# Memory norm on rows, four chunks of seven products in the first values unit, queries turned by DMA, two changes of order

## The chip, the cores and the metric

The kernel runs on one core of a Trainium2 chip. A core has a matrix engine (TensorE; in the profile PE, and PEld for its weight loads), a vector engine (VectorE, DVE), a scalar engine (ScalarE, ACT), a general engine (GpSimd, POOL) and a queue engine (SyncE, SP) that issues DMA transfers. The metric is the time of one execution on the device in microseconds (us), as a median of several runs.

## The reference

One decoder layer, batch 1, 256 tokens, width 2048, all in fp32:

```
h = x + 0.5 * SwiGLU_1(rmsnorm(x))                  # 2048 -> 5632 -> 2048
z = rmsnorm(h) @ w_in                               # columns u, v (1024 each), q (1024), k and v of the window (256)
h = h + concat(rmsnorm(gate(u, v)), rmsnorm(window_attention(q, k, v))) @ w_out
kv = rmsnorm(mem, g_mem) @ w_xkv                    # memory of 256 rows: keys 2048, values 2048
h = h + cross_attention(rmsnorm(h) @ w_xq, kv) @ w_xo
h = h + 0.5 * SwiGLU_2(rmsnorm(h))
out = rmsnorm(h)

rmsnorm(x, g) = x * rsqrt(mean(x*x, -1) + 1e-5) * g
```

The factor `rsqrt(mean(mem*mem)+eps)` is one number for each row of the memory. It can multiply the normalised memory before the product with `w_xkv`, or the rows of the product behind it.

## The kernel before, in words

**Products.** Each fp32 operand is split into a high part (fp32r) and the rest: ACT casts the high part, DVE subtracts it to get the low part (`split`, L146 to L148). A product of two such operands is three matmuls: high by high, low by high, high by low. In the names of the profile `wh` and `wl` are high and low parts of a weight, `th` and `tl` those of sums of weights, `fh` and `fl` those of a pair of the left operand.

**Units and chunks.** A projection of 256 tokens onto 1024 columns is a *unit*: 2 x 2 output blocks of 128 tokens by 512 columns, each a PSUM bank, over the 2048 rows of the weight. The weight comes in 8 *chunks* of 256 rows (1 MB, `load`, L347). A chunk is a product of 2 x 2 by 2 x 2 blocks and comes in kinds. `N` and `C` use eight block products (24 matmuls, L447); `S` uses Strassen's seven (21 matmuls) on sums of the blocks of both operands. The left operand's blocks and sums lie in a `Pair` (L190). The sums of the weight's blocks (`t`, L356 to L360) are made by DVE for each `S` chunk. Kind `D` is a pair with the sums of both `S` and `C`, so that one unit may use it as the one and another unit as the other; its extra forms are called `more`.

**Order on PE.** PE's order is the order of the program. `push` (L513) loads a chunk and hands its matmuls to `turn` (L505), which first issues the matmuls of the chunk before (`flush`), so that loading and splitting run one chunk ahead. `turn` then calls the functions in `later` whose count is 0, and counts the rest down. Functions in `side` (norms, transposes, attention) are generators that `side_step` continues between every six matmuls.

**Order on the other engines.** ACT, DVE, POOL and SP instructions are ordered by a planner that goes by the order of the program and by when it expects each operand. Every engine then runs its instructions in that order and waits at the head. Weights wait for one of three raw buffers and one of two `wh` and `wl` buffers; a DMA on SP's queue holds up those behind it while it waits for its source.

**Places that the change touches.**

- First layer, start: `first_pair` (L906) makes pairs of `n1` from raw rows of x transposed: ACT scales the rows (L936) and casts, DVE subtracts (L148). The pair's sums (`sums`, L924, `fill_sums`, L272) aren't wanted before the second unit; they are put off by `later`.
- Queries: `late_q` (L982) scales the rows of the query projection, `queries` (L990) turns them on PE with 16 transposes in the stage of the window's keys and values (`narrow_unit`, L551; 96 matmuls of 256 columns at L571) and copies four banks. `attend` (L1077) needs them after.
- Memory norm: `beside_queries` sums the squares of the memory's rows; `spread` (L1009) turns the factor of each row into a tile `by_token` that has it along the free dimension, by a product with a matrix of ones. `pair_normalized` (L306) multiplies the transposed memory by gain and `by_token` on DVE, for eight pairs `mT`.
- Memory values and keys: units `mv0`, `mv1` (L1255, L1259) and `mk0`, `mk1` (L1307). Their seven-product chunks are closed by `seven_early` and `seven_late` (L593, L601) on DVE, which write the rows.
- Output projection of the cross attention: `added_unit("xo", ...)` (L676), twice, with side work that turns the next norm's input through PSUM banks of the pool `tr`. Its seven-product chunks open the banks P1, Q5, Q6 and Q7 in the same pool.
- `turned_rows` (L150), used elsewhere already: ACT copies rows so that the two 16-bit halves of each word stand apart, a transposing DMA on SP's queue turns them, and ACT joins the halves afterwards.

## Time and profile before

| | |
|---|---|
| median of 3 runs | 2025.03 us (2024.72 to 2027.14) |
| profiled execution | 2024.46 us, its span 2022.8 us |
| PE busy | 2007.2 us, 9165 matmuls recorded |
| PEld, DVE, ACT busy | 82%, 92%, 65% of the span |
| granted clock of PE | 0.999 |
| mean DMA rate | 206 GB/s |

Starts of stages on PE, in us: first layer 6; query projection 694; keys and values 739; v 753; u 800; first values 853, second 906; keys 952 and 995; output of the mixer 1038; cross queries 1127; cross output 1228; second layer 1331 to 2014.

A row of time has start, duration, engine, line, operation, output and inputs, shapes, and in brackets how long the engine was idle before it and for what. A matmul's duration overlaps the next one's, so distances between starts tell the pace. A group row has count, total busy time and the mean of one in ns. A row of windows has, for each engine, busy time and number of instructions.

### The profile page before, as it was taken

What the parts mean: (1) busy time and instruction counts of PE and PEld (TensorE: products, weight loads), DVE (VectorE), ACT (ScalarE), POOL (GpSimd) and SP (SyncE); (2) the same over time, 40 slices, a digit from 0 to 9 for tenths busy, and PEclk for the clock granted to TensorE, in tenths of its full rate; (3) what the DMA queues carried; (4) which work ended last, traced back from release to release, by engine and by line L of the source; (5) the groups of instructions that cost most, each with busy time, mean ns of one, the idle gap of its engine ahead of it and who ended that gap; (6) DMA issues with size and microseconds to landing.
All of it is one profiled execution on the core that took longest, in us unless ns stands there. A gap on an engine that the chain in (4) does not pass through costs nothing.

```text
span 2022.8 us, 24182 instructions
## 1 busy us (share of the span) xinstructions
PE 2007.2 (99%) x9165; PEld 1665.3 (82%) x9165; DVE 1859.3 (92%) x1993; ACT 1305.5 (65%) x1442; POOL 34.0 (2%) x57
## 2 busy tenths in 40 slices
PE   9999999999999999999999999999999999999998
PEld 7888888888888888888888888888888888888886
DVE  7999999989999978988878977899999999999998
ACT  7656666667765766655556676675666665676664
POOL 0000000000000010100000000000000000000000
PEclk9999999999999999999999999999999999999999
DMA  8676657666555565545665544456576657565563
GB/s 313 202 242 208 222 207 234 214 218 219 191 205 208 189 227 198 185 159 187 210 217 185 203 150 151 177 188 235 194 236 221 224 196 242 203 219 203 189 227 125
DMA packets 115333, 415.83 MB, mean 206 GB/s; under 512 B 61824, under 2 KB 63888, under 8 KB 68112
## 3 DMA queue, kind: packets, MB, share of 16 engines
q1 hardware_dynamic: 112768, 407.14, 57.5%
q0 software_dynamic: 2016, 6.30, 1.0%
q8 instruction: 72, 1.18, 0.2%
q10 hardware_dynamic: 432, 0.84, 0.1%
q14 instruction: 45, 0.37, 0.1%
HBM read 398.52 MB, written 2.10 MB: 198 GB/s over the span
## 4 chain that ended last, share of the span: by engine, by line
PE 73%; DVE 3%; issue 1%; ACT 1%; POOL 0%; POOLq 0%; DVEq 0%
PE f2gQ L447 16%; PE f2dQ L447 6%; PE f1dQ L447 6%; PE f2gP L447 6%; PE xqQ L447 3%; PE f2dP L447 3%; PE f1dP L447 3%; PE woQ L447 2%; PE xoQ L447 2%; PE f2dR L447 2%; PE f1dR L447 2%; PE mv0Q L447 2%; PE vQ L447 2%; PE mv1Q L447 2%; PE mk1Q L447 2%; PE mk0Q L447 2%
## 5 line engine op out<-in xcount | busy, mean ns | idle before, releaser
L147 ACT CAST f2gwh<-f2gw 128x1536 fp32r<-128x1536 f32 (+1 forms) x88 | 150.6, 1712 | 76.0 <-PE f2gQ L447 58.8
L147 ACT CAST f1gwh<-f1gw 128x1536 fp32r<-128x1536 f32 (+2 forms) x94 | 152.1, 1622 | 67.4 <-PE f1gQ L447 51.9
L148 DVE TENSOR_TENSOR f1gwl<-f1gw,f1gwh 128x1536 fp32r<-128x1536 f32 (+2 forms) x94 | 181.4, 1931 | 14.3 <-ACT f1gwh L147 14.1
L148 DVE TENSOR_TENSOR f2gwl<-f2gw,f2gwh 128x1536 fp32r<-128x1536 f32 (+1 forms) x88 | 179.4, 2040 | 6.7 <-ACT f2gwh L147 6.6
L447 PE MATMUL f2gQ<-f2gwh,n4fh 128*128 128x512 f32 x317 | 123.6, 390 | 0.0
L447 PE MATMUL f2gQ<-f2gwh,n4fl 128*128 128x512 f32 x317 | 123.4, 389 | 0.0
L447 PE MATMUL f1gQ<-f1gwh,n1fl 128*128 128x512 f32 x315 | 122.7, 389 | 0.0
L447 PE MATMUL f1gQ<-f1gwh,n1fh 128*128 128x512 f32 x315 | 122.6, 389 | 0.0
L147 ACT CAST f2gth<-f2gt 128x1024 fp32r<-128x1024 f32 x82 | 85.1, 1049 | 57.8 <-DVE f2gt L356 29.4
L147 ACT CAST f1gth<-f1gt 128x1024 fp32r<-128x1024 f32 x78 | 81.1, 1049 | 60.5 <-DVE f1gt L356 30.7
L147 ACT CAST f2dwh<-f2dw 128x2048 fp32r<-128x2048 f32 (+1 forms) x44 | 77.4, 1758 | 48.0 <-PE f2dQ L447 43.2
L147 ACT CAST f1dwh<-f1dw 128x2048 fp32r<-128x2048 f32 (+1 forms) x44 | 77.4, 1758 | 41.0 <-PE f1dQ L447 37.3
L148 DVE TENSOR_TENSOR f1dwl<-f1dw,f1dwh 128x2048 fp32r<-128x2048 f32 (+1 forms) x44 | 92.3, 2098 | 11.4 <-ACT f1dwh L147 11.2
L148 DVE TENSOR_TENSOR f2dwl<-f2dw,f2dwh 128x2048 fp32r<-128x2048 f32 (+1 forms) x44 | 92.3, 2097 | 11.0 <-ACT f2dwh L147 10.7
L148 DVE TENSOR_TENSOR f2gtl<-f2gt,f2gth 128x1024 fp32r<-128x1024 f32 x82 | 99.8, 1221 | 1.3 <-ACT f2gth L147 0.3
L447 PE MATMUL f2gQ<-f2gwl,n4fh 128*128 128x512 f32 x317 | 96.7, 390 | 0.0
L447 PE MATMUL f1gQ<-f1gwl,n1fh 128*128 128x512 f32 x315 | 96.4, 390 | 0.0
L148 DVE TENSOR_TENSOR f1gtl<-f1gt,f1gth 128x1024 fp32r<-128x1024 f32 x78 | 95.2, 1221 | 1.1
L447 PE MATMUL f1gP<-f1gwh,n1fl 128*128 128x512 f32 x176 | 68.8, 391 | 2.2 <-DVE n1fl L148 2.1
L447 PEld LDWEIGHTS f2gQ<-f2gwh,n4fl 128*128 128x128 f32 x317 | 59.5, 188 | 12.3
L447 PEld LDWEIGHTS f2gQ<-f2gwh,n4fh 128*128 128x128 f32 x317 | 59.5, 188 | 12.3
L447 PEld LDWEIGHTS f2gQ<-f2gwl,n4fh 128*128 128x128 f32 x317 | 59.4, 188 | 12.3
(790 smaller groups left out, 6026.2 us busy)
## 6 DMA issues: line engine op xcount, KB each, us to landing
f2gw<-in_w_gu SPq DMA_DIRECT2D x88, 1024.0 KB, 4.9
f1gw<-in_w_gu SPq DMA_DIRECT2D x86, 1024.0 KB, 5.1
f1dw<-in_w_down SPq DMA_DIRECT2D x44, 1024.0 KB, 4.8
f2dw<-in_w_down SPq DMA_DIRECT2D x44, 1024.0 KB, 4.8
wow<-in_w_out SPq DMA_DIRECT2D x16, 1024.0 KB, 4.9
xqw<-in_w_xq SPq DMA_DIRECT2D x16, 1024.0 KB, 4.8
xow<-in_w_xo SPq DMA_DIRECT2D x16, 1024.0 KB, 4.8
qw<-in_w_in SPq DMA_DIRECT2D x8, 1024.0 KB, 4.7
```

The source lines that it names most:

```text
L147: nc.scalar.copy(hi, src)
L148: nc.vector.tensor_tensor(lo, src, hi.bitcast(F32), ALU.subtract)
L447: nc.tensor.matmul(self.banks[name], x, y, start=name not in self.begun, stop=self.left[name] == 0)
```

## The change

Five edits in one:

1. The pairs of the memory are scaled by the gain alone, on ACT (`pair_scaled`); `spread` and `by_token` are gone. The row's factor is applied to the finished rows of values and keys, on ACT (`rows_scaled`), four times for each of the four units.
2. The first pair of the memory becomes kind `D` with forms of its own; the first values unit has four chunks of seven products in place of three, with its chunks in another order.
3. The queries are turned by `turned_rows` and joined on ACT, called through `later`.
4. In the units `xo`, the first chunk of seven products issues the bank Q6 last, and each term's three matmuls together.
5. In the first layer the sums of pairs 0 and 1 are put off by three turns in place of two, and pair 2's by two in place of one.

```diff
                 if kind == "D":
+                    tag = "mTmore" if s == "mT" else "more"
                     self.more = [
-                        const.tile([P, 2, P], F32R, tag="more" + t, name=nm(s + "more")) for t in "hl"
+                        const.tile([P, 2, P], F32R, tag=tag + t, name=nm(s + "more")) for t in "hl"
                     ]
...
-    def pair_normalized(s, kind, raw, i, gcol, by_token):
-
-        turned = 1 if kind in "SD" else 0
+    def pair_scaled(s, kind, raw, i, gcol):
+
         for k in range(2):
             c = gcol + 2 * i + k
             o = row_tile(kind, raw, k)
-            nc.vector.scalar_tensor_tensor(
-                out=o, in0=o, scalar=sm[:, c:c + 1], in1=by_token[:, turned:turned + 2, :],
-                op0=ALU.mult, op1=ALU.mult,
-            )
+            nc.scalar.activation(o, o, AF.Copy, scale=sm[:, c:c + 1])
         p = Pair(s, kind)
         fill(s, p, raw)
...
+            whole = by_bank
+            if kind == "S" and self.last_bank and self.last_bank not in self.begun:
+                order = sorted(order, key=lambda x: x[0] == self.last_bank)
+                whole = True
...
-                    last = steps if by_bank or (kind == "S" and bn[0] == "B") else behind
+                    last = steps if whole or (kind == "S" and bn[0] == "B") else behind
...
-    KINDS_M = "CCSCSCSC"
+    KINDS_M = "DCSCSCSC"
...
         u = Unit(s, kinds, LATE_O, clear=True)
+        if s == "xo":
+            u.last_bank = "Q6"
...
-            later.append((1 if i in (2, 3) else 2, sums))
+            later.append(((3, 3, 2, 1)[i] if i < 4 else 2, sums))
...
-        side_add(queries())
-
-    def queries():
         for j in range(2):
-            qt = m4("qT").rearrange("p (c t) -> p c t", c=4)
-            for c in range(0, 4, 2):
-                yield 1 if j or c else 4
-                pt = bank("qTp")
-                for i in range(2):
-                    for tb in range(TB):
-                        col = (j * 4 + c + i) * P
-                        nc.tensor.transpose(
-                            pt[:, (i * TB + tb) * P:(i * TB + tb + 1) * P],
-                            qs[tb][:, col:col + P], ident,
-                        )
-                nc.scalar.copy(qt[:, c:c + 2, :], pt.rearrange("p (c t) -> p c t", c=2))
-            qT[j] = qt
+            later.append((j, lambda j=j: queries(j)))
+
+    def queries(j):
+        t = tile_turned("qt")
+        for tb in range(TB):
+            turned_rows("q", t[:, tb], qs[tb][:, j * 512:(j + 1) * 512])
+
+        def joined():
+            qt = m4("qT")
+            words = words_of(qt, 8)
+            for tb in range(TB):
+                nc.scalar.copy(words[:, tb::2], by_block(t)[:, tb])
+            qT[j] = qt.rearrange("p (c t) -> p c t", c=4)
+
+        later.append((1, joined))
...
-            side_add(spread())
+            rsm.append(rstd_of(partsm, NG, D))
...
-            mT[i - 2] = pair_normalized("mT", KINDS_M[i - 2], loaded.pop(), i - 2, G_MEM, by_token)
+            mT[i - 2] = pair_scaled("mT", KINDS_M[i - 2], loaded.pop(), i - 2, G_MEM)
...
-    def late_mv0(ps):
+    def rows_scaled(at):
         for name, tb, j in BLOCKS:
-            nc.scalar.copy(mv[j][:, tb * 512:(tb + 1) * 512], ps[tb, j])
-
-    seven_unit(
-        "mv0", FEWER, w_xkv, 2, mT, lambda tb, j: mv[j][:, tb * 512:(tb + 1) * 512],
-        beside=lambda i: beside_mT(8 + i) if i < 2 else None, order=(0, 2, 1, 3, 4, 5, 6, 7),
-    )
-    seven_unit("mv1", FEWER, w_xkv, 3, mT, lambda tb, j: mv[2 + j][:, tb * 512:(tb + 1) * 512])
+            nc.scalar.activation(at(tb, j), at(tb, j), AF.Copy, scale=rsm[0][:, tb:tb + 1])
+
+    def values(cb, kinds, **more):
+        def at(tb, j):
+            return mv[2 * cb + j][:, tb * 512:(tb + 1) * 512]
+
+        seven_unit(f"mv{cb}", kinds, w_xkv, 2 + cb, mT, at, lambda: rows_scaled(at), **more)
+
+    values(0, MORE, beside=lambda i: beside_mT(8 + i) if i < 2 else None, order=(1, 0, 3, 2, 5, 4, 6, 7))
+    values(1, FEWER)
...
-        def late(ps=None):
-            if ps is not None:
-                for name, tb, j in BLOCKS:
-                    nc.scalar.copy(kr[j][tb], ps[tb, j])
+        def late():
+            rows_scaled(lambda tb, j: kr[j][tb])
```

`MORE` is "SCSCSCSC" and `FEWER` is "CCSCSCSC"; `fill`, `row_tile`, `words_of`, `by_block` and `tile_turned` are as before.

More of the change, by code (lines that the diff above doesn't have):

```diff
@@ L399, in __init__ @@
             self.gate_first = False
+            self.last_bank = None
             self.begun = set()
@@ L987, in late_q @@
             )
-        side_add(queries())
-    def queries():
         for j in range(2):
-            qt = m4("qT").rearrange("p (c t) -> p c t", c=4)
-            for c in range(0, 4, 2):
-                yield 1 if j or c else 4
-                pt = bank("qTp")
-                for i in range(2):
-                    for tb in range(TB):
-                        col = (j * 4 + c + i) * P
-                        nc.tensor.transpose(
-                            pt[:, (i * TB + tb) * P:(i * TB + tb + 1) * P],
-                            qs[tb][:, col:col + P], ident,
-                        )
-                nc.scalar.copy(qt[:, c:c + 2, :], pt.rearrange("p (c t) -> p c t", c=2))
-            qT[j] = qt
-    seven_unit("q", "CCCSCCSC", w_in, 2, n2, None, late_q, beside_queries)
-    by_token = const.tile([P, 3, P], F32, name="by_token")
-    def spread():
-        rsm = rstd_of(partsm, NG, D)
-        yield 2
-        dg = s2("dg")[:, :T].rearrange("p (b t) -> p b t", b=TB)
-        for tb in range(TB):
-            nc.vector.tensor_scalar_mul(dg[:, tb, :], ident, rsm[:, tb:tb + 1])
-        yield 4
-        ps = bank("by_token")[:, :T]
-        for tb in range(TB):
-            nc.tensor.matmul(ps[:, tb * P:(tb + 1) * P], ones, dg[:, tb, :], start=True, stop=True)
-        nc.scalar.copy(by_token[:, :2, :].rearrange("p b t -> p (b t)"), ps)
-        nc.scalar.copy(by_token[:, 2, :], ps[:, :P])
+            later.append((j, lambda j=j: queries(j)))
[10 more added lines that the diff above has]
+        later.append((1, joined))
+    seven_unit("q", "CCCSCCSC", w_in, 2, n2, None, late_q, beside_queries)
+    rsm = []
     kd, vv = [], []
```

## The prediction

> **What bounds the kernel now.** I read the profile's page first, then the waits of the matrix engine (PE), then the order of time at each place that the change touches.
>
> ```profile
> span 2022.8 us, 24182 instructions
> PE 2007.2 (99%) x9165; PEld 1665.3 (82%) x9165; DVE 1859.3 (92%) x1993; ACT 1305.5 (65%) x1442; POOL 34.0 (2%) x57
> ```
>
> PE is never idle for long, so a product taken out is worth its issue interval, and a wait of PE is worth its length. The list of PE's waits (total, times, longest) has two that matter:
>
> ```profile
> PE f1gP L447 <- DVE n1fl L148: 2.1, 1, 2.1
> PE xoQ L447 <- ACT n4r L267: 1.2, 1, 1.2
> ```
>
> Starts of products are closer together than their busy times, so I count by starts. PE's order of time in the second half of the output projection:
>
> ```profile
> 1303.47 0.39 PE L447 MATMUL xoP<-xowh,xofh 128*128 128x512 f32 x1
> ...
> 1306.19 0.39 PE L447 MATMUL xoQ<-xoth,xofl 128*128 128x512 f32 x1
> 1307.75 0.50 PE L447 MATMUL xoQ<-xoth,xofh 128*128 128x512 f32 x1 [1.17 <-ACT n4r L267]
> ```
>
> From 1303.47 to 1306.19 are 12 intervals: 0.227 us each for a product of 512 columns. The next one took 1.56, which is 1.33 too many.
>
> **The change, part by part.** I count gains against the profiled execution.
>
> *Products.* The first values unit gets four chunks of 7 products in place of three: 24 - 21 = 3 matmuls fewer, 0.68 us. Its price is on DVE, below.
>
> *The bank Q6.* The chunk that begins at 1303.47 issues P1, P2, Q3 with three matmuls each, then two each for Q5, Q7, Q6: Q6's first is its 14th, and it waits for the bank that ACT reads at L267. Put last, with every term's three matmuls together, it is the 19th: due at 1303.47 + 18 x 0.227 = 1307.55 instead of 1306.42. The wait ended at 1307.75, so 0.20 is left and 1.13 is gained. Ends: 0, if the reading slips with it, and 1.44 (1.33 and a restart of 0.11, as at 26.20 below), if it comes earlier. I take 1.13, by the row. The low halves of the T sums are now wanted at the 12th product, not the 18th; DVE had stored them before this chunk's second third:
>
> ```profile
> 1303.25 1.22 DVE L148 TENSOR_TENSOR xotl<-xot,xoth 128x1024 fp32r<-128x1024 f32 x1
> ```
>
> 1303.25 + 1.22 = 1304.47, against 1303.47 + 11 x 0.227 = 1305.97. If that cover went, each microsecond late would be one lost.
>
> *The sums of the first layer's pairs.* PE, DVE, then ACT, at the start:
>
> ```profile
> 23.36 0.39 PE L447 MATMUL f1gP<-f1gwh,n1fh 128*128 128x512 f32 x1
> 25.86 0.50 PE L447 MATMUL f1gP<-f1gwh,n1fl 128*128 128x512 f32 x1 [2.10 <-DVE n1fl L148]
> 26.20 0.40 PE L447 MATMUL f1gP<-f1gwh,n1fh 128*128 128x512 f32 x1
> ```
>
> ```profile
> 21.97 2.29 DVE L148 TENSOR_TENSOR f1gwl<-f1gw,f1gwh 128x2048 fp32r<-128x2048 f32 x1 [0.92 <-ACT f1gwh L147]
> 24.18 0.68 DVE L148 TENSOR_TENSOR n1fl<-n1f,n1fh 128x512 fp32r<-128x512 f32 x1
> ...
> 25.11 1.29 DVE L148 TENSOR_TENSOR n1fl<-n1r,n1fh 128x512 fp32r<-128x512 f32 x2
> ```
>
> ```profile
> 17.64 2.50 ACT L936 ACTIVATE n1r<-n1r,sm 128x256 f32<-128x256 f32 x6
> 20.04 1.89 ACT L147 CAST f1gwh<-f1gw 128x2048 fp32r<-128x2048 f32 x1
> ```
>
> PE loses (25.86 - 23.36 - 0.23) + (26.20 - 25.86 - 0.23) = 2.38. It waits for pair 3's low half (25.11), which stands behind two operations of pair 0's sums (24.18 to 25.11: 0.93) and a weight subtraction, itself behind ACT's cast at 20.04 and six row scalings, two of them pair 0's (2.50 x 2/6 = 0.83). Pair 0's and 1's sums now come one chunk later and pair 2's too, so both go from here: at least 0.93 + 0.83 = 1.76 back; 2.38 if the low half also passes the weight's subtraction. I take 1.8, the end that needs no change of order. The work isn't gone: sums of pairs 1, 2 and 3 now fall in one turn, a chunk later, and what is late next is the low half and the weight of the fifth or sixth chunk. Then the gain is 0 (rival 1); I know no reason for a loss.
>
> *Queries turned by DMA, and no by_token.* The keys and values stage:
>
> ```profile
> 738.76 0.28 PE L571 MATMUL kv<-kvwh,n2fh 128*128 128x256 f32 x1
> ...
> 741.51 0.28 PE L571 MATMUL kv<-kvwl,n2fh 128*128 128x256 f32 x1
> ...
> 752.69 0.40 PE L447 MATMUL vP<-vwh,n2fh 128*128 128x512 f32 x1
> 752.92 0.40 PE L447 MATMUL vP<-vwh,n2fl 128*128 128x512 f32 x1
> 753.32 0.50 PE L447 MATMUL vP<-vwl,n2fh 128*128 128x512 f32 x1
> ```
>
> 23 intervals in 2.75 us are 0.1196 each. The stage has 96 products, 11.48 us; it lasts 13.93. So 2.45 us go to the 16 transposes, the two by_token products and their restarts, and all go.
>
> ```profile
> L999 PE MATMUL qTp<-ident,qs x16: 270/272/328, 741.6 to 745.7; 128*128 128x128 f32 x16
> ```
>
> By these durations the transposes alone would be 16 x 0.272 = 4.4 us, more than the stage has to give; the starts decide. The Trainium skill ("TensorE: Matmul & The Clock Gate", Part 4: PE-mode transpose) states about 275 ns for a transpose within a kernel, which agrees with the duration; taken as the price it would make the forecast some 2 us lower.
>
> In their place come four ACT copies, four transposing DMAs on SP's queue, and two more pairs of ACT copies once these land, against four 0.59 us bank copies. The same helpers run in the first layer (ns, least/median/most):
>
> ```profile
> L153 ACT COPY f1w<-f1gp x10: 1035/1037/1047, 97.6 to 469.0; 128x1024 uint16<-128x1024 uint16 x10
> L156 SPq DMA_TRANSPOSE f1a<-f1w x22: 1237/1244/2755, 58.1 to 471.3; - x22
> ```
>
> Queued behind a copy on ACT are the casts of kvwh and vwh; behind a transpose on SP, the loads of vw; behind the joining copies, the next vwh.
>
> ```profile
> 738.74 1.91 ACT L147 CAST kvwh<-kvw 128x2048 fp32r<-128x2048 f32 x1 [0.35 <-PE qQ L447]
> 740.55 0.72 ACT L985 ACTIVATE qs<-qv,rs 128x512 f32<-128x512 f32 x1
> ...
> 746.57 1.90 ACT L147 CAST vwh<-vw 128x2048 fp32r<-128x2048 f32 x1
> ```
>
> ```profile
> 740.96 2.28 DVE L148 TENSOR_TENSOR kvwl<-kvw,kvwh 128x2048 fp32r<-128x2048 f32 x1
> 749.83 1.23 DVE L356 TENSOR_TENSOR vt<-vw 128x1024 f32<-128x1024 f32 x1 [6.59 <-DMA vw<-in_w_in]
> 750.97 2.29 DVE L148 TENSOR_TENSOR vwl<-vw,vwh 128x2048 fp32r<-128x2048 f32 x1
> ```
>
> ```profile
> 743.27 0.33 SPq L354 DMA_DIRECT2D vw<-in_w_in  x1
> ```
>
> A copy in ACT's gap at 738.4 (ends 739.4) lets two scalings of qs through first (2 x 0.72, to 740.9), and kvwh then ends at 742.8, kvwl at 745.1. PE wants kvwl at its 51st product, 738.76 + 50 x 0.1196 = 744.74: 0.4 lost, 1.4 with a second copy ahead. I take 0.6. The values unit is then due at 752.69 - 2.45 + 0.6 = 750.84, its third product at 751.3. That one waits today for vwl, which DVE issues behind vt, that is behind a load which starts only when kvwl frees its buffer (743.27) and takes 6.56. The order was a near tie: vwh ended at 748.47, the load at 749.83. After the change the load starts later (745.1, plus 1.24 per transpose ahead) and vwh need not wait for bank copies: I expect vwl ahead of vt, ending about 750.2, with nothing lost and today's 0.28 (753.32 and its restart) saved. Gain 2.45 - 0.6 + 0.3 = 2.1; the other end is rival 2.
>
> *The memory norm.* DVE loses 16 multiplications, ACT gets 16 scalings of 256 columns, about 0.45 each (n1r above: 2.50/6):
>
> ```profile
> L312 DVE SCALAR_TENSOR_TENSOR mTr<-mTr,sm,by_token x16: 474/482/485, 804.1 to 858.0; 128x256 f32<-128x256 f32 x16
>   ACT mTfh L147: 7.3, 5
> ```
>
> ACT stood idle 7.3 us for just these, about what it now works: nothing. Without that cover it is up to 7.2 us on ACT. The first pair's extra forms add some 2 us of DVE. Each of the four units gets four more ACT scalings of 0.72 (as qs), 2.9 us at its end, waiting for DVE's last sums; queued behind is the next unit's cast:
>
> ```profile
> 904.75 1.90 ACT L147 CAST mv1wh<-mv1w 128x2048 fp32r<-128x2048 f32 x1 [2.44 <-PE mv0Q L447]
> ```
>
> ACT was idle 2.44 before it, and a chunk of 24 products (5.4 us) passes before PE wants it: nothing; 4 x 2.9 if that cover went. The fourth chunk of sevens costs DVE:
>
> ```profile
> 853.00:905.00 52.00, 52.00 (x262) 43.90 (x261) 44.33 (x59) 26.98 (x35) 0.00 (x0) 1.00 0.47 170
> ```
>
> ```profile
> L148 DVE TENSOR_TENSOR vwl<-vw,vwh x8: 1753/2284/2293, 751.0 to 788.6; 128x2048 fp32r<-128x2048 f32 x5, 128x1536 fp32r<-128x1536 f32 x3
> ...
> L356 DVE TENSOR_TENSOR vt<-vw x3: 1215/1224/1225, 749.8 to 775.4; 128x1024 f32<-128x1024 f32 x3
> L359 DVE TENSOR_TENSOR vt<-vt,vw x3: 681/683/685, 753.2 to 777.1; 128x512 f32<-128x512 f32 x3
> ```
>
> A chunk of sevens takes 1.75 + 1.22 + 2 x 0.68, and two more subtractions of 1024 columns, by L356 1.22 each: 6.77 against 2.28, so 4.49 more. DVE (the third number after the window's length, 44.33 of 52) loses about 2 of multiplications and gains 4.49: some 47 of 51, which PE still hides. I take 0, between 0 and a loss of 4.5 (rival 3).
>
> **Sum.** 0.68 + 1.13 + 1.8 + 2.1 = 5.7 us. The profiled execution took 2024.46 around its span of 2022.8, 0.57 under the median of 2025.03; so 2018.8 for it, and 2019.3 for a median.
>
> **Rivals.** *1. The start's stall only moves.* For it: DVE has hardly a gap from 21.97 to 26.4, and three pairs' sums now share a turn. Against: a chunk of PE is 5.4 us, its weight subtraction 2.29 and its low half 0.69, so DVE gets ahead by over 2 us a chunk. The 1.8 are lost: 2021.1.
>
> *2. The values unit (v) waits for SP; slower than before.* DVE keeps vt ahead of vwl, as today, and vw's load starts late: kvwl at 746.1 with two copies ahead of its cast, two transposes ahead on SP (2 x 1.24), 748.6; the load 6.56, vt 1.22, vwl 2.29: 758.7, where it is 753.26 today. PE's third product is then 5.4 later than before and not 2.1 earlier: 2019.3 + 7.5 = 2026.8. It makes the whole slower from the point where vwl ends later than 753.3 + 3.6 = 756.9, the 3.6 being the other three gains. For it: today's order, and the longest issue of a transpose in this trace, 2.755. Against: the near tie of 748.47 and 749.83, which both edits push apart in the other direction.
>
> *3. DVE is the bound in the first values unit.* All 4.49 show on PE: 2023.8. For it: sevens come at the second and fourth chunk, where DVE also serves attention. Against: PE issues its products at an even 0.227 through chunks of sevens. The Trainium skill ("Perfetto Trace Analysis", Identifying the Most-Contended Engine) says that matmul busy time tells little of headroom, and that weight-load share and the other engines' occupancy do: by that DVE's 92% here stands above the weight loads' 82%, and this rival would be the likely one. The even starts speak against it.
>
> *4. The bank isn't freed in time by the order.* If ACT's reading slips with PE, Q6 waits as long as now: 1.13 lost, 2020.4; part of the forecast's own range.
>
> **How the numbers follow.** Forecast 62% (rival 4 in it; its own range 2017.8 to 2020.9), rival 1 13%, rival 2 12%, rival 3 9%, others 4%. A measurement here tells about 0.2% from no change: 2021.0 and 2029.1 are the bounds. Faster: the forecast nearly whole and, as 2021.1 stands at the bound, half of rival 1: 66%. Slower by that much takes more than rival 2's price: with the others 6%. Within: 28%. The range 2017.6 to 2024.5 holds the forecast, rivals 1 and 3 and most of a rival 2 that stays small; below it lies only what both ends of the start (0.6) and of the bank (0.3) could add.
>
> **What would show it.** Start: no wait of PE for n1fl over 0.5 us near 23.4, and none new before 55. Keys and values: no L999 and L1019, the stage near 12 us, vwl ahead of vt on DVE, no gap over 0.4 at the values unit's third product. Bank: a wait of about 0.2 ahead of Q6. First values unit: 180 products, starts at 0.227 throughout. It is wrong if PE waits over 2 us for a weight or a low half in a place where it doesn't now, or if the list of PE's waits shows the old two at their old length.

## The result, and the profile after

The changed kernel takes 2022.1 us as a median of 20 runs (2021.12 to 2023.72). In the same comparison the kernel before takes 2025.67 us (20 runs, 2024.11 to 2028.61). The ratio is 0.9983, with a 95% interval from 0.9977 to 0.9989: some 3.5 us, or 0.17%. The forecast was 2019.3 us, a gain of 5.7, with 2017.8 to 2020.9 as its own range; the result lies outside that, within the wide range (2017.6 to 2024.5), 1 us above rival 1, and on the no-change side of the 0.2% bound, while a gain beyond that bound had been given 66%. The profiled span fell from 2022.8 to 2019.4 us. That difference is near the one of the medians, so the two profiles can be taken apart by stages, but partly by luck: the changed kernel's profiled execution (2021.12 us) is the shortest of its 20, 0.98 below its median, and the one of the kernel before (2024.46) lies 1.21 below the 2025.67.

The head of the page of the changed kernel:

```profile
span 2019.4 us, 24193 instructions
PE 2005.4 (99%) x9142; PEld 1662.6 (82%) x9142; DVE 1858.4 (92%) x1984; ACT 1329.5 (66%) x1479; POOL 34.0 (2%) x57
```

ACT has 24 us more to do, PE 1.8 less. The table gives the length of each stage, from its first product to the next stage's first product, worked out from the starts in the two traces. Stages that are not named agree within 0.03 us. The output of the cross attention is counted here from the attention's products in the bank xo, at 1199.8 us, on, and not from the projection's first product at 1228.

| stage | before | after | gain | predicted |
|---|---|---|---|---|
| first layer's gate unit and up (with the start) | 455.68 | 456.04 | -0.36 | 1.8 |
| first layer's down projection | 232.55 | 232.39 | 0.16 | 0 |
| keys and values of the window | 13.93 | 11.51 | 2.42 | 2.1 with v |
| v | 47.21 | 46.78 | 0.43 | |
| u | 52.76 | 53.11 | -0.35 | 0 |
| memory values, two units | 99.66 | 98.94 | 0.72 | 0.68 |
| memory keys, second unit | 42.94 | 43.77 | -0.83 | 0 |
| output of cross attention | 130.99 | 129.89 | 1.10 | 1.13 |

The gains add up to 3.29; the first product starts 0.09 earlier, which makes 3.38 of the 3.4.

**The start.** PE's waits of the changed kernel (total, times, longest):

```profile
PE f1gP L450 <- DVE f1gwl L148: 1.3, 1, 1.3
...
PE f1gP L450 <- ACT f1gwh L147: 0.8, 1, 0.8
PE mk1Q L450 <- DVE yafl L142: 0.6, 1, 0.6
```

The wait of 2.1 for n1fl is gone. The first row is new. A row of 0.8 for f1gwh stands in the list of the kernel before too, but there it is the first product's, at 6.00; here it is one at 40.65. In PE's order of time:

```profile
39.22 0.61 PE L450 MATMUL f1gQ<-f1gwl,n1fh 128*128 128x512 f32 x2
40.65 0.50 PE L450 MATMUL f1gP<-f1gwh,n1fh 128*128 128x512 f32 x1 [0.82 <-ACT f1gwh L147]
40.98 0.39 PE L450 MATMUL f1gP<-f1gwh,n1fl 128*128 128x512 f32 x1
...
46.47 0.39 PE L450 MATMUL f1gP<-f1gwh,n1fl 128*128 128x512 f32 x1
48.11 0.50 PE L450 MATMUL f1gP<-f1gwl,n1fh 128*128 128x512 f32 x1 [1.26 <-DVE f1gwl L148]
48.45 0.40 PE L450 MATMUL f1gP<-f1gwh,n1fh 128*128 128x512 f32 x1
```

From 39.45 (the second of the pair in the first row) to 40.65, and from 46.47 to 48.11: with the restarts 2.62 us are lost, where the kernel before lost 2.38 at 23.4. What is late first is ACT's cast of the seventh chunk (38.70 to 40.60), then DVE's low part of the eighth. The eighth's own cast ends at 44.25, but DVE comes to the low part at 45.77 only, since the seventh's low part was late and sums of pairs and of a weight (42.91 to 45.77) stand between. DVE, then ACT:

```profile
40.63 2.29 DVE L148 TENSOR_TENSOR f1gwl<-f1gw,f1gwh 128x2048 fp32r<-128x2048 f32 x1 [1.04 <-ACT f1gwh L147]
...
44.30 1.22 DVE L353 TENSOR_TENSOR f1gt<-f1gw 128x1024 f32<-128x1024 f32 x1
...
45.77 2.28 DVE L148 TENSOR_TENSOR f1gwl<-f1gw,f1gwh 128x2048 fp32r<-128x2048 f32 x1
```

```profile
33.79 0.63 ACT L137 ACTIVATE junk<-h 128x512 f32<-128x512 f32 x1
...
37.05 0.62 ACT L137 ACTIVATE junk<-h 128x512 f32<-128x512 f32 x1
37.57 0.19 ACT L137 ACTIVATION_READ_ACCUMULATOR junk<-h 128x1 f32 x1
37.66 0.60 ACT L147 CAST n1fh<-n1f 128x512 fp32r<-128x512 f32 x1
38.17 0.62 ACT L147 CAST n1fh<-n1r 128x512 fp32r<-128x512 f32 x1
38.70 1.90 ACT L147 CAST f1gwh<-f1gw 128x2048 fp32r<-128x2048 f32 x1
```

The rows called junk are squares of x for the first norm: eight of them, with their sums 8 x (0.62 + 0.19) = 6.4 us of ACT between 33.8 and 42.4, which my working never mentioned.

**Keys and values.** The queue of SP and DVE's order around the first chunk of v:

```profile
738.70 6.00 SPq L156 DMA_TRANSPOSE qt<-qw  x2
744.80 0.53 SPq L351 DMA_DIRECT2D vw<-in_w_in  x1
745.37 5.47 SPq L156 DMA_TRANSPOSE qt<-qw  x2
```

```profile
747.15 2.29 DVE L148 TENSOR_TENSOR vwl<-vw,vwh 128x2048 fp32r<-128x2048 f32 x1 [3.73 <-ACT vwh L147]
751.05 1.22 DVE L353 TENSOR_TENSOR vt<-vw 128x1024 f32<-128x1024 f32 x1 [1.61 <-DMA vw<-in_w_in]
752.19 0.60 DVE L1036 TENSOR_SCALAR kd<-kv,rs 128x128 f32<-128x128 f32 x2
```

The order of vwl and vt is turned round, as forecast, and PE has no wait there. But SP is held up longer than the two times 1.24 for each pair of transposes. The row of 6.00 us isn't all issue: SP issues one transpose for 1.25, waits from 739.95 to 743.44 for the next rows that ACT copies, and issues the second for 1.26, with the load of vw behind it. The pair of 5.47 has no such wait; its issues take 1.66 and 3.77 (ns, least/median/most of the four):

```profile
L156 SPq DMA_TRANSPOSE qt<-qw x4: 1253/1463/3765, 738.7 to 747.1; - x4
```

So the next load of vw starts at 750.94, vt follows at 751.05, and the scalings of the values' rows (L1038) behind that. PE wants the bank of these rows at v's 13th product, and there this profile had luck: it loses 0.07 us, the six other profiles with this order lose 0.39 to 1.55.

**Bank Q6.** In the second half of the cross output PE's starts are 1305.06 and then 1305.49, so 0.43 - 0.23 = 0.20 is left of 1.33:

```profile
1305.06 0.39 PE L450 MATMUL xoQ<-xotl,xofh 128*128 128x512 f32 x1
1305.49 0.50 PE L450 MATMUL xoQ<-xoth,xofh 128*128 128x512 f32 x1
```

**Second keys unit.** One wait that wasn't there: PE wants a bank that DVE is still to read for the mixer's turned rows (yafl), and DVE does a weight's low part first. DVE's and PE's order of time:

```profile
1004.33 2.28 DVE L148 TENSOR_TENSOR mk1wl<-mk1w,mk1wh 128x2048 fp32r<-128x2048 f32 x1
1006.53 0.90 DVE L142 SCALAR_TENSOR_TENSOR yafl<-ya,sm,yafh 128x256 fp32r<-128x256 f32 x2
```

```profile
1007.16 0.47 PE L450 MATMUL mk1Q<-mk1th,mTfh 128*128 128x512 f32 x1 [0.60 <-DVE yafl L142]
```

In the kernel before DVE read these banks before the low part:

```profile
1005.77 0.48 DVE L142 SCALAR_TENSOR_TENSOR yafl<-ya,sm,yafh 128x256 fp32r<-128x256 f32 x1
...
1007.59 0.48 DVE L142 SCALAR_TENSOR_TENSOR yafl<-ya,sm,yafh 128x256 fp32r<-128x256 f32 x1
1007.99 2.28 DVE L148 TENSOR_TENSOR mk1wl<-mk1w,mk1wh 128x2048 fp32r<-128x2048 f32 x1
```

### The profile page after: what moved, and what is told of

Read it like the earlier page. It is cut to its first block, busy times and chain, and to the rows that moved or that the text cites. A ratio compares the mean times of both kernels' runs of the same rounds, so it can differ in the third digit from the quotient of the medians.

```text
span 2019.4 us, 24193 instructions
## 1 busy us (share of the span) xinstructions
PE 2005.4 (99%) x9142; PEld 1662.6 (82%) x9142; DVE 1858.4 (92%) x1984; ACT 1329.5 (66%) x1479; POOL 34.0 (2%) x57
## 3 DMA queue, kind: packets, MB, share of 16 engines
q8 instruction: 72, 1.18, 0.2%
## 4 chain that ended last, share of the span: by engine, by line
PE 93%; DVE 3%; ACT 2%; issue 1%; DMA 1%; SPq 0%; POOL 0%; POOLq 0%; DVEq 0%; ACTq 0%
PE f2gQ L450 16%; PE f1gQ L450 15%; PE f2dQ L450 6%; PE f1dQ L450 6%; PE f2gP L450 6%; PE f1gP L450 5%; PE xqQ L450 3%; PE f2dP L450 3%; PE f1dP L450 3%; PE woQ L450 2%; PE xoQ L450 2%; PE f2dR L450 2%; PE f1dR L450 2%; PE vQ L450 2%; PE mv1Q L450 2%; PE mk0Q L450 2%
## 5 line engine op out<-in xcount | busy, mean ns | idle before, releaser
L450 PEld LDWEIGHTS f1gQ<-f1gwl,n1fh 128*128 128x128 f32 x315 | 59.1, 188 | 12.7 <-DVE f1gwl L148 0.4
L450 PE MATMUL f1gP<-f1gwh,n1fh 128*128 128x512 f32 x176 | 68.7, 391 | 0.8 <-ACT f1gwh L147 0.8
```

What stands on the lines that cost most here:

```text
L450: nc.tensor.matmul(self.banks[name], x, y, start=name not in self.begun, stop=self.left[name] == 0)
```

## The experiments

Stage lengths of all kernels in us, from their traces as in the table above (gate is the first layer's gate stage, mv both memory values units, mk1 the second keys unit, xo the cross output). These are single profiled executions; only the two last kernels were timed in several rounds.

| kernel | gate | kv | v | u | mv | mk1 | xo | span |
|---|---|---|---|---|---|---|---|---|
| before | 455.68 | 13.93 | 47.21 | 52.76 | 99.66 | 42.94 | 130.99 | 2022.8 |
| after | 456.04 | 11.51 | 46.78 | 53.11 | 98.94 | 43.77 | 129.89 | 2019.4 |
| sums undone | 457.28 | 11.51 | 47.45 | 53.11 | 98.94 | 43.78 | 129.87 | 2021.2 |
| squares later | 460.39 | 11.51 | 47.14 | 53.13 | 98.94 | 44.04 | 129.89 | 2025.7 |
| sums apart | 460.81 | 11.51 | 48.27 | 53.13 | 98.94 | 43.77 | 129.89 | 2025.8 |
| mk1 bank | 455.99 | 11.51 | 47.59 | 53.09 | 98.94 | 42.94 | 129.90 | 2019.9 |
| queries only | 455.40 | 12.61 | 47.56 | 52.76 | 99.65 | 45.10 | 131.00 | 2023.9 |
| norm only | 455.80 | 13.49 | 47.82 | 52.76 | 99.65 | 43.78 | 131.00 | 2023.8 |
| sums 3322 | 455.98 | 11.51 | 47.09 | 53.13 | 98.94 | 42.94 | 129.89 | 2020.2 |
| sums 3332 | 458.93 | 11.51 | 47.15 | 53.09 | 98.94 | 42.94 | 129.89 | 2022.0 |
| no squares | 453.14 | 11.51 | 47.87 | 53.11 | 98.94 | 43.77 | 129.91 | 2018.7 |
| four sums less | 454.78 | 11.51 | 47.63 | 53.13 | 98.94 | 43.79 | 129.89 | 2020.1 |
| bank and queries | 456.20 | 11.51 | 46.99 | 53.07 | 98.94 | 42.94 | 129.90 | 2020.1 |
| squares on GpSimd | 467.11 | 11.51 | 48.87 | 53.07 | 98.94 | 42.94 | 129.91 | 2034.2 |

My first theories of the start were: A, the squares of x on ACT stand ahead of the casts; B, three pairs' sums in one turn hold VectorE; C, neither.

### Sums undone

```
-            later.append(((3, 3, 2, 1)[i] if i < 4 else 2, sums))
+            later.append((1 if i in (2, 3) else 2, sums))
```

> The changed kernel with the sums of the first layer's pairs put back to their turns of before. Theory A (the start's wait was only moved, since ACT's squares of x and row scalings stand ahead of the casts of the seventh and eighth chunk) and theory B (it was moved because the sums of pairs 1, 2 and 3 now fall in one turn) both expect the wait of 2.1 us for n1fl near 23.4 back, no wait near 39.5 and 46.5, and the first layer's second product to begin at 461.7, 0.3 earlier than with the sums put off. If instead the waits near 39.5 and 46.5 come on top of the old one (theory C: they come from somewhere else in the change), it begins near 464.

The old wait is back at its old length (23.16 to 25.66, 2.50 between starts), and none follows it before 55. Theory C is out: the second product of the layer (the down projection) begins at 463.06 us, 461.5 without the 1.6 explained below. But the stage is 1.6 us longer than the kernel before's, which has the same wait. Windows of this kernel (length, busy time and count of PE, PEld, DVE, ACT, POOL, then PE's granted clock, DMA share, GB/s):

```profile
23.00:26.00 3.00, 0.89 (x5) 0.42 (x4) 3.00 (x5) 3.00 (x5) 0.00 (x0) 1.00 1.07 407
26.00:30.00 4.00, 4.00 (x12) 3.14 (x11) 4.00 (x8) 2.00 (x6) 0.00 (x0) 0.57 1.02 387
```

After the wait the clock was granted at 0.57, and eight products came 0.427 us apart in place of 0.227: 8 x 0.20 = 1.6. In the kernel before's profile the clock stayed at 1.00. So at the same clock this kernel's stage is 457.28 - 1.6 = 455.7 us, the kernel before's, and the change of order gained nothing there.

### Squares later, and sums apart

```
-        for j in {5:(0,1),6:(2,3)}.get(i, ()):
+        for j in {6:(0,1),7:(2,3)}.get(i, ()):
...
-        if i == 6:
+        if i == 7:
             rs1.append(rstd_of(parts1, NG, D))
```

> The changed kernel with the eight squares of x one chunk later (beside chunks 6 and 7 in place of 5 and 6). Theory A (ACT's squares ahead of the cast) expects the wait of 0.8 us for f1gwh near 39.5 gone, and that near 46.5 gone or smaller: 1 to 2.4 us gained by the end of the first unit. Theory B (the burst of sums) expects both waits to stay within 0.3 us.

```
-            later.append(((3, 3, 2, 1)[i] if i < 4 else 2, sums))
+            later.append((3 if i < 4 else 4, sums))
```

> The changed kernel with the sums of the eight pairs each in a turn of its own (one pair a chunk from the fourth turn on), so that no turn has three. Theory B (the burst) expects the waits near 39.5 and 46.5 gone, 2.4 us gained. Theory A (ACT's squares) expects the wait near 39.5 to stay, since the squares stand where they stood, with at most 0.6 us less for one cast of sums that leaves the queue.

Both took some 6 us more than the changed kernel, which no theory had; 4.4 and 4.8 of it lie in the gate stage, most of the rest in v and the second layer. At the start both did better than the changed kernel: the products that it begins at 54.63 begin at 53.78 with the squares later and at 52.71 with the sums apart. That is less than either theory wanted (A 1 to 2.4 us from the squares, where 0.85 came; B 2.4 from the sums, where 1.92 came and the wait at 39.5 stayed, at 0.66 lost). The loss comes later. In the list of PE's waits of the kernel with the sums apart, and in PE's order of time of the one with the squares later:

```profile
PE f1gQ L450 <- DVE f1gtl L148: 2.9, 8, 1.0
```

```profile
107.52 0.61 PE L450 MATMUL f1gQ<-f1gtl,n1fh 128*128 128x512 f32 x2
108.41 0.73 PE L450 MATMUL f1gQ<-f1gtl,n1fh 128*128 128x512 f32 x2 [0.28 <-DVE f1gtl L148]
```

The second product of the pair is due at 107.74 + 0.23 and starts at 108.41; with its restart that is 0.55, and it comes again every 41.4 us, eight times up to 398. DVE is busy 97% of this stage in the changed kernel (393.03 us of 405 between 55 and 460), and in these two kernels the planner gave it another order from there to the stage's end: of the changed kernel's 353 operations between 62 and 459 us only 251 and 255 come in the same sequence. So an edit to a few operations at 35 us decided, by the order that the planner found, over 4 us in the next 400. What the two edits are worth by themselves can't be told from their stages; in the kernels that follow, DVE's order there is nearly the changed kernel's (342 to 353 of the 353).

### Bank Q6 in the second keys unit

```
         u = Unit(s, kinds, alone=alone, sparse=True)
+        if s == "mk1":
+            u.last_bank = "Q6"
```

> The changed kernel with the bank Q6 put last in the first chunk of seven products of the second keys unit as well. If the wait of 0.6 us there (0.93 with its restart) is one for a bank that DVE still reads for the mixer's turned rows, it goes: Q6 comes five products (1.13 us) later; the stage of the second keys unit shortens from 43.76 to about 42.9. If the wait is for an operand (the low parts of the sums of weights), it stays or grows, since these are wanted earlier.

The wait is gone from the list, and the unit takes 42.94 us again: 0.83 back. The span is 0.5 longer than the changed kernel's all the same, since the first product came 0.28 later, v took 0.8 more and the down projection 0.3.

### Queries only, and norm only

```
-        side_add(queries())
...
+            later.append((j, lambda j=j: queries(j)))
...
```

> The kernel before with the queries turned by DMA and nothing else; by_token stays, so its two products and its group on PE stay. If the queries' edit is worth what the stages of the changed kernel show, the stage of the first key and value rows falls from 13.93 to about 11.9 us (11.48 of products and some 0.4 for by_token), and the start (the wait at 23.4, 2.4 us) and the xo wait of 1.3 us stay as before. In the changed kernel and the three experiments on its start, v's third product waited 0.07, 0.7, 0.7, 0.2 and 1.4 us for the scaling of the values' rows. Theory SP (the two transposing transfers of the second half hold SP some 5.5 to 6.5 us, v's next weights land late behind them, and the scaling stands behind the sum of those weights on VectorE) expects here too a wait of 0 to 1.4 us at v's third product and the second half's transfers between two of v's loads on SP. Its rival (the wait comes from the clock of the memory norm's path, so from edit 1) expects none here.

```
-            nc.vector.scalar_tensor_tensor(
-                out=o, in0=o, scalar=sm[:, c:c + 1], in1=by_token[:, turned:turned + 2, :],
...
+            nc.scalar.activation(o, o, AF.Copy, scale=sm[:, c:c + 1])
...
-    seven_unit("mv1", FEWER, w_xkv, 3, mT, lambda tb, j: mv[2 + j][:, tb * 512:(tb + 1) * 512])
...
+    values(1, FEWER)
...
```

> The kernel before with the memory norm's factor on the rows of keys and values and nothing else: by_token and its group are gone, the first values unit keeps three chunks of seven products, queries on TensorE, old sums, old bank order. Theory norm (the two small losses of the changed kernel come from the new row scalings: 0.36 us in u because the attention's exponentials stand later on ACT, 0.83 us in the second keys unit at its third product) expects both here: u longer by 0.3 to 0.4 us than 52.76 and a wait of about 0.6 us (1.08 from product to product) for the mixer's turned rows in the second keys unit. The rival (they come from the shift of everything by the queries' transfers) expects u at 52.8 and no such wait. By_token's end is worth 0.3 to 0.5 us in the stage of the first rows either way, the first values unit stays at 183 products, and start and xo stay as before.

The stage of the keys and values is 1.32 shorter with the queries alone and 0.44 with the norm alone, but 2.42 with both. With the queries alone by_token's products now wait themselves, which hid behind the transposes before:

```profile
PE mk1Q L447 <- DVE yafl L142: 1.3, 1, 1.3
...
PE by_token L1018 <- DVE dg L1014: 0.4, 1, 0.4
```

The first of these rows settles the second keys unit. Each edit alone brings the wait for yafl: 2.16 us of the unit with the queries, 0.84 with the norm. Each takes a side group off PE, and so, it seems, the mixer's group that comes after it meets other work; the rows show the meeting, not that it came about in this way. The norm's scalings aren't needed for it, since the queries' edit has none. The 0.35 us in u comes with neither alone. It is there in every kernel with both; in the changed kernel 0.24 of it is at one transpose of the attention (pT, at 820.58, 0.348 from start to start, where its neighbours take 0.11). Its cause is open. With the norm's scalings and three chunks of sevens mv stays at 99.65, so the 0.72 come with the fourth chunk and its order. With the norm alone v lasts 47.82 although the queries are still turned on PE, so not all of v's spread is due to the transposing DMAs.

### The sums two turns and three turns apart

```
-            later.append(((3, 3, 2, 1)[i] if i < 4 else 2, sums))
+            later.append(((3, 3, 2, 2)[i] if i < 4 else 2, sums))
...
-            later.append((j, lambda j=j: queries(j)))
+            later.append((2 * j, lambda j=j: queries(j)))
```

Both also have the bank of the second keys unit; the other kernel has (3, 3, 3, 2).

> The changed kernel with three edits in three stages: the sums of the fourth pair one turn later (two pairs a turn in place of three), the second half of the queries turned one turn later, and bank Q6 last in the second keys unit. After the two experiments that moved the squares or all the sums, the order of VectorE in the whole first gate stage was another and cost some 0.55 us per pair of units, eight times; here that order is the changed kernel's from the second unit on, so no wait is expected between 60 and 460 us. Start: theory B (three pairs' sums in one turn hold VectorE, so the eighth chunk's low part is late) expects the wait at 46.5 (1.65 us from product to product) to go, and the one at 39.5 (1.2 us, a cast on ACT behind the squares of x) to stay: the gate stage shorter by 1.0 to 1.5 us. Theory A (the squares alone) expects both to stay within 0.3 us. Queries: theory SP expects no wait for the values' rows at v's third product, v at 46.7 us or less from its first product to u's; if the second half is then late for the attention, u or v grows by up to 1 us. Second keys unit: 42.9 us as in the experiment on the bank alone.

> As the kernel with the fourth pair's sums one turn later, but with the third's one turn later still, so that turns hold one, one and three pairs. Theory B expects the waits at 39.5 and 46.5 to shrink as the three-pair turn moves behind the eighth chunk, and, if anything, a wait at the start of the second unit (51 to 62 us), where the sums are first read; the gate stage is then between the changed kernel's 456.0 us and 2 us less. Theory A expects the wait at 39.5 to stay at 1.2 us. v and the second keys unit as in its sister: no wait for the values' rows, 42.9 us.

Theory B has fallen. With (3, 3, 2, 2) the wait at 39.5 is gone and the one at 46.5 has grown to all of it:

```profile
45.45 0.39 PE L450 MATMUL f1gP<-f1gwh,n1fl 128*128 128x512 f32 x1
47.99 0.50 PE L450 MATMUL f1gP<-f1gwl,n1fh 128*128 128x512 f32 x1 [2.15 <-DVE f1gwl L148]
```

That's 2.54 between starts, 2.31 lost (2.42 with the restart), and the stage is 455.98 where the changed kernel's was 456.04. With (3, 3, 3, 2) PE loses 1.40 at 39.75 and 2.02 at 56.02, and then the clock drops again:

```profile
54.00:59.00 5.00, 3.14 (x14) 2.31 (x13) 5.00 (x6) 4.85 (x6) 0.00 (x0) 1.00 0.81 252
59.00:62.50 3.50, 3.50 (x11) 2.71 (x10) 3.50 (x4) 1.05 (x1) 0.00 (x0) 0.51 0.96 286
```

Without those eight slow products its stage would last 457.3 us. So with the sums moved by a turn the loss stays at 2.3 to 3.4 us (restarts left out), and A as I had put it (the place of the squares) can't be all either. What is left is the amount of work: in the 16 us after 34, ACT and DVE of the changed kernel work 13.97 and 13.92 us. The kernel with the sums apart agrees: up to the product that begins at 52.71 there it lost less than the changed kernel, and it had put off more work past it, 5 of the 16 operations of the sums in place of 1.

The queries' edit took the wait at v's 13th product away in both (v 47.09 and 47.15; with the changed kernel's order seven profiles gave 46.8 to 48.3, 47.6 in the middle).

### Work left out: squares, then sums

```
-                square_into(parts1[:, tb, j:j + 1], h[:, tb, j * 512:(j + 1) * 512], 512)
+                if j == 0:
+                    nc.gpsimd.memset(parts1[:, tb], 512.0)
```

> The changed kernel without the eight squares of x and their sums (6.4 us of ACT between 33 and 43 us); a constant stands for the sums of the squares, so the first norm's factor is wrong, and no other work is left out. The order of VectorE in the gate stage is the changed kernel's from the second unit on. Theory total of ACT (the first unit loses about 2.4 us wherever the sums are put, because ACT's casts of weights stand behind work that has to be done in these 50 us) expects the waits at 39.5 and 46.5 to shrink by most of 2.6 us and the gate stage at 453.5 to 454.3 us in place of 456.0. Theory total of VectorE (its halves of the sums and of the weights are what is late, ACT has time) expects at most 0.8 us off, 455.2 us or more.

```
-            later.append(((3, 3, 2, 1)[i] if i < 4 else 2, sums))
+            if i in (2, 3, 4, 5):
+                n1[i].sums = n1[i - 2].sums
+            else:
+                later.append(((3, 3, 2, 1)[i] if i < 4 else 2, sums))
```

> The changed kernel without the sums of the third to the sixth pair of x, which use those of the pair two before (its products are wrong by that): 12 instructions and some 5 us of VectorE less, 2 us of casts on ACT less; the squares stay. Theory total of ACT expects the wait at 39.5 behind the squares to stay near 1.2 us and the gate stage at 455.0 us or more. Theory total of VectorE expects both waits to go and the gate stage at 453.5 to 454.3 us. If both kernels give 2 us or more, the two engines' work is in series there (a cast on ACT, then the low part on VectorE) and neither alone is the bound.

Windows of the changed kernel, of the one without squares and of the one with four sums less:

```profile
20.00:34.00 14.00, 14.00 (x63) 11.59 (x62) 12.00 (x19) 11.73 (x18) 0.00 (x0) 1.00 1.04 400
34.00:50.00 16.00, 13.93 (x60) 10.87 (x59) 13.92 (x22) 13.97 (x27) 0.83 (x1) 1.00 0.54 194
```

```profile
34.00:50.00 16.00, 16.00 (x73) 13.24 (x72) 15.77 (x19) 10.36 (x13) 0.00 (x0) 1.00 0.68 253
```

```profile
34.00:50.00 16.00, 15.33 (x68) 12.39 (x67) 12.56 (x14) 12.33 (x22) 0.73 (x1) 1.00 0.69 260
```

Without the squares PE doesn't stop at all after the first chunks: 73 products in these 16 us in place of 60, and a stage of 453.14 us, 2.90 less. ACT's casts of the weights come at 36.08 and 39.97, not 38.70 and 42.35. With four sums less the stage is 1.26 shorter: the wait at 46.5 is gone and the one behind the squares stays (39.86 to 40.92, 0.83 lost). From 30 us on this kernel loses 0.95 in place of 2.62; its first chunks, which the edit doesn't touch, happened to take 0.5 more. The size lies between what the two theories wanted for this kernel; which of the two waits stays speaks for ACT. The changed kernel's loss is thus ACT's work ahead of its casts, and without the squares it is gone. The sums' own part on ACT and DVE makes the second wait. For the kernel before this isn't shown: its wait at 23.4 lies ahead of its first square (27.49), and no run leaves the squares out with the old order.

### Both mends, timed; and the squares on GpSimd

```
+        if s == "mk1":
+            u.last_bank = "Q6"
...
-            later.append((j, lambda j=j: queries(j)))
+            later.append((2 * j, lambda j=j: queries(j)))
```

> The changed kernel with bank Q6 last in the second keys unit and the second half of the queries turned one turn later; the start as in the changed kernel. From the two experiments with these edits: second keys unit 42.94 in place of 43.77 us, v at 47.1 us with little spread in place of 46.8 to 48.3 us. Expected against the changed kernel: 0.8 us from the keys and 0 to 0.7 us from v on the median, so about 2020.7 to 2021.3 us where the changed kernel's median was 2022.1 us, ratio to the kernel before about 0.9975 to 0.9980. If v's spread does not come from the transfers on SP, the spread of this kernel's times stays at 2.6 us and its median at 2021.3 us.

2021.9 us, median of 11 runs (2021.24 to 2023.62), beside 2025.54 for the kernel before on that chip; ratio 0.9982, from 0.9973 to 0.9991. Against the changed kernel's 0.9983 that is no difference that can be told, and the 2020.7 to 2021.3 us that were expected didn't come. The 0.83 of the keys unit is there in the profile, but more went elsewhere: 0.7 at the first layer's down projection (233.11 us for 232.39), where PE waits for a sum on DVE, and 0.37 in the cross queries (73.21 for 72.84), where the trace has a new wait. v lasts 46.99. The spread of the times is 2.4 us, hardly less than the changed kernel's 2.6, so the wait at v's 13th product, which this kernel doesn't have, isn't what makes most of it.

```
-            for tb in range(TB):
-                square_into(parts1[:, tb, j:j + 1], h[:, tb, j * 512:(j + 1) * 512], 512)
+            part = h[:, :, j * 512:(j + 1) * 512]
+            o = m4("sq").rearrange("p (b d) -> p b d", b=TB)
+            nc.gpsimd.tensor_tensor(o, part, part, ALU.mult)
+            if squares:
+                nc.gpsimd.tensor_tensor(o, o, squares[-1], ALU.add)
+            squares.append(o)
...
```

> The version with bank Q6 last in the second keys unit and the second half of the queries one turn later, and the squares of x moved from ACT to GpSimd, which has nothing else to do there: four products of 128x1024 by themselves, three additions, and one sum over the row on VectorE. Theory total of ACT expects what leaving the squares out gave: no wait at 39.5 and 46.5, the gate stage near 453.1 to 453.6 us, 2.4 to 3 us less than in the changed kernel, and the median near 2019.2 us (2021.9 less 2.7), ratio to the kernel before about 0.9970. It falls short if GpSimd needs more than some 2.5 us an operation: the sum on VectorE then stands at the head of its queue and PE waits there, and the gain is given back; and if GpSimd and VectorE slow one another, the low parts between 26 and 42 us take longer than 2.29 us.

2033.04 us, ratio 1.0037 (1.0023 to 1.005): slower by 7 us. GpSimd was done at 43.5, so it wasn't late. But while it worked, DVE did hardly anything. GpSimd's and DVE's order of time:

```profile
31.74 2.45 POOL L957 TENSOR_TENSOR sq<-sq,sq 128x1024 f32<-128x1024 f32 x1
34.15 2.34 POOL L955 TENSOR_TENSOR sq<-h 128x1024 f32<-128x1024 f32 x1
36.57 2.40 POOL L957 TENSOR_TENSOR sq<-sq,sq 128x1024 f32<-128x1024 f32 x1
```

```profile
31.87 2.88 DVE L148 TENSOR_TENSOR n1fl<-n1r,n1fh 128x512 fp32r<-128x512 f32 x1
34.66 2.11 DVE L148 TENSOR_TENSOR n1more<-n1d,n1more 128x256 fp32r<-128x256 f32 x1
36.70 2.55 DVE L278 TENSOR_TENSOR n1f<-n1r 128x256 f32<-128x256 f32 x1
...
43.71 0.41 DVE L278 TENSOR_TENSOR n1f<-n1r 128x256 f32<-128x256 f32 x1
```

The same subtraction of 256 columns takes 2.55 us beside GpSimd and 0.41 after it. Each of DVE's operations ends 0.3 to 0.6 us after one of GpSimd's: they take turns. PE then waits 7.6 us, up to 41.54, for ACT's cast of a weight, which stands behind the cast of a pair's sums that DVE finished at 39.25. After that wait the clock is granted at 0.50 up to 45.95, and ten products come 0.43 us apart, which costs some 2 us more. v lasts 48.87 here, although the second half of the queries comes later: so that edit doesn't always hold v's start. Whether the 2.9 us can be kept with the squares done elsewhere is open.

## Why the prediction was right and wrong, step by step

- **Products, 0.68:** right, 0.72 over both units. The first is 1.63 shorter and the second 0.91 longer, because eight of the attention's products (sv) now fall behind the border. The norm alone leaves the two units as they were, so the gain is the fourth chunk's. Rival 3 (DVE the bound there) didn't come: DVE works 46.74 of the 51.26 us of the first unit, and PE loses nothing. The rule of the Trainium skill ("Perfetto Trace Analysis", Identifying the Most-Contended Engine) that was weighed beside it would have named DVE; the even starts were the better sign.
- **Bank Q6, 1.13:** right, 1.10, with the 0.20 of wait that was forecast.
- **Queries and by_token, 2.1:** right, though not by the way in which it was added up. The stage gave 2.42 and v 0.43 in this profile, 2.85 in all. The 0.43 are luck: with the 47.6 us that v lasts in the middle of the seven profiles with this order v loses 0.4, and 2.0 are left. The 0.6 set down for a late kvwh didn't come: one copy stood ahead of its cast, which began 0.47 later than before, and PE had that to spare. The order of vwl and vt turned round as said. By the price of a transpose that the Trainium skill states ("TensorE: Matmul & The Clock Gate", Part 4: PE-mode transpose), PE should have got 4.4 us and more back; the distances between starts were right. SP's part was mis-sized: one of the four issues took 3.77 us and not 1.24, and SP stood 3.5 us between the first two. Rival 2 came in a small form in the other profiles, as 0.39 to 1.55 us lost at v's 13th product.
- **Sums of the first layer's pairs, 1.8: this step failed.** I took the wait at 23.4 for the price of an order and asked what would be late next, but only on DVE, by its gaps up to 26.4. It was rival 1, given 13%. The stall moved to 39.5 and 46.5, and 2.62 us were lost there in place of 2.38. "DVE gets ahead by over 2 us a chunk" left out that DVE waits for ACT's cast and that ACT has the squares of x to do at 33.8, 6.4 us. The runs show that no order that was tried ends this stage before 455.4 us, that the two which began it better lost more later, and that taking the squares off ACT gives 453.1. Why the order of before, with its wait ahead of the squares, ends at the same time isn't shown.
- **Memory norm, 0:** wrong by 0.83 in the second keys unit, and perhaps by the 0.35 in u. The covers that were named did hold: no cast came late, no product waited for a scaling. What wasn't named is that with a group less on PE the later groups, and DVE's order with them, may fall elsewhere. The queries alone lose there too, and more (2.16).

By the table: 5.7 predicted; the start brings 2.16 less, u and the second keys unit 1.18 less, keys and v 0.75 more, the down projection 0.16 more: 3.3. The second keys unit wasn't among the rivals at all. The range's lower end, 2017.6, had no term either: with both ends named for the start and the bank the forecast goes down to 2018.4 only.

## What to carry to other kernels

A wait at the start of a kernel can be a debt of work and not of order, as it was here: before a stall is counted as gained, add up what every engine in the chain (here ACT, then DVE, then PE) still has to do before PE gets ahead, with work that has nothing to do with the stall. Where a planner orders the engines, an edit that removes or moves a small group can shift the groups behind it, so look for buffers that are read late in stages that the diff doesn't touch, and compare the engines' order over whole stages before an experiment is believed. An idle engine isn't free if it shares something with a busy one.

## What the runs showed of the hardware

**A wait of some 2.3 to 2.5 us can cost 1.6 us more.** Six profiles have a wait of PE between 2.25 and 2.54 us from start to start in the first layer. In two of them the granted clock fell afterwards to about half (0.57 and 0.51 in the windows above), and eight products came 0.427 us apart; in the other four it stayed at 1.00. A seventh, the one with the squares on GpSimd, waited 7.98 and ran at 0.50 for 4.4 us. Most of the timed executions fit this. Beside the last two kernels the kernel before was timed 24 times: ten executions with a mean granted clock of 0.999 took 2023.33 to 2025.12 us, fourteen with 0.998 took 2025.21 to 2027.95. (Of two single ones earlier 2026.41 at 0.998 fits and 2023.19 at 0.998 doesn't.) The changed kernel's twenty, with no wait over 1.65 us at the start, show no such split: 2021.12 to 2023.41 at 0.998, 2021.63 to 2023.72 at 0.999. The medians of the two groups lie 2.0 us apart, so by an estimate 14/24 of that, some 1.1 us, of the gain of 3.5 may be a drop of the clock that the changed order avoids, which no step of the prediction had. That the drop was at this wait in those executions isn't shown, since only the profiled ones tell where it was. The Trainium skill ("TensorE: Matmul & The Clock Gate", Part 1: The HAM clock gate) says that an idle array falls to half its clock and needs a busy window of some 3.4 us to come back, and that this window runs freely. Eight products of 0.427 are 3.4 us, which agrees; the page speaks of an idle window of the same 3.4 us, while here 2.3 to 2.5 us were enough two times in six.

**GpSimd and VectorE took turns.** A subtraction of 0.41 us took 2.55 beside GpSimd's products and sums of 2.07 to 2.45. The Trainium skill ("GPSIMD Engine Reference", Key points) says that the two share their ways to SBUF and contend when VectorE has two inputs there. The trace agrees, and it shows the size: of the 2.55 us VectorE lost 2.1.

**A transposing DMA can hold its queue much longer than its usual issue.** Of the four that turn the queries three took SP 1.25 to 1.66 us, and the last, issued right behind another, 3.77, against 1.24 for most in the first layer. The load of vw behind it could start at 750.94 only. In the kernel with the second half a turn later, two in a row took 1.24 and 1.32, so it isn't the row of two by itself that makes the long one.
